# A priority for the split of the weights in a hybrid encoder step

## The chip, the cores and the metric

The kernel runs on one core of one Trainium2 chip. The metric is the device time of one execution in microseconds; a kernel's time is the median over several executions. The profile is one further execution, taken by the hardware profiler. The engines are called as the profile calls them: PE (TensorE) with its weight loads PEld, DVE (VectorE), ACT (ScalarE), POOL (GpSimd), SP (SyncE, which issues nearly all DMAs, all in one queue).

## The reference

One layer of a streaming encoder, for 2048 new frames with 16 learned meta tokens ahead of them and for 64 frames of a running stream:

```
h = RMSNorm(x); p = h @ W_in
o = concat[DiffAttn(p_A), RG-LRU(p_B), GLA(p_C)] @ W_out; x = x + o
h = RMSNorm(x)
x = x + (gelu(causal_dwconv3(h @ W_up)) * (h @ W_gate)) @ W_down
y = RMSNorm(x)
```

The model width is 1024, the width of the feed-forward part (FFN) 2816. Differential attention has 4 heads with two softmaxes each, under a mask that is causal by chunks of 64; RG-LRU and GLA are recurrences along the tokens. Everything is in float32.

## The kernel before

**Precision by splitting.** A float32 operand of a large product is split into two float32r parts, `hi` (the value rounded) and `lo` (the rest), and a product is three matmuls: hi·hi, lo·hi, hi·lo. So every weight tile of 128x1024 is split before it is used: it is loaded from HBM into `raw` (2 buffers), ACT rounds it into `whi` (line 154), and POOL (line 260, two of three) or DVE (line 160, one of three) subtracts to get `wlo`. `whi` and `wlo` have 3 buffers each.

**The list of weight pieces.** `parts` names the pieces in the order of their use: 86 for the projection W_in, then for each of three token groups the pieces of W_out, W_up, W_gate and W_down. The first two groups have 512 tokens each, the last 1104 in three blocks. In the first group a piece of W_out, W_up, W_gate or W_down is split as described, and its two halves are also stored to HBM (`WS`); in the second and third group they are loaded from `WS` and nothing is split. So there are 160 splits, 86 in the projection and 74 in the first group, and 148 pairs of loads from `WS`.

**When a piece is made ready.** `w_pump` is called between the products of the dense stream, `w_take` where a piece is used; both call `w_split`, which runs at most 3 pieces ahead of those used up (`NW`), so the buffer that a piece gets is that of the piece three places ahead of it in the list. `w_split` also calls `w_load`, the next load into `raw`.

**The order on the engines.** Three streams are written down interleaved, by estimated costs: the dense stream (projection, W_out, FFN), the attention and the recurrences. Each instruction has a priority number, the running `tc.cur_priority` at the place where it was written; a scheduler then orders each engine's instructions along a simulated time line, and of those that could start, the smallest number goes first. The streams get offsets by which they stand ahead: attention 30000, the recurrences 16000, the dense stream 0, the norms inside the dense stream 50000, the start of the program 100000 (`FIRST`). The last group runs alone, after the other streams. The streams end at:

```
    flow.run((dense(), 1875e3, 0), (attention(), 560e3, 30000),
             (recurrent(), 616e3, 16000))
```

**Names used below.** PE: `ps_w` the projection (lines 644, 646), `pd` W_out (line 1437) and W_down (line 1369), `pu` and `pg` W_up and W_gate (line 1302), `ps_sc` the attention scores (lines 1055, 1062), `ps_pt` transposes and `ps_o` the products with V (line 1169). The scores go through the minimum `NB` on DVE (line 1064) and the exponential `pc` on ACT (line 1065); `ph` is a transposed piece of the probabilities on ACT (line 154). `ck` and `ckr` are cached keys and their split, `e_gv` evictions of the projection, `Q`, `Kc`, `V` the loads of the attention.

Of the kernel before, what the change touches and what calls it, by code (L numbers as in the profile page):

```python
# [105 lines left out]
def f(ap):  # L106
    return ap.bitcast(F32)
# [31 lines left out]
def tile_hymba_step(ctx, tc, xT, xkT, cache_v, wi, wo, wu, wg, wd, par, sgla, c_msk, yT_p, yT_s, nkT_p, nv_p, lh_p, lc_p, gs_p, fc_p,  # L139
# [4 lines left out]
    def raw32(ap):  # L144
        return ap.bitcast(F32) if ap.dtype == F32R else ap

    def ld(out, in_):
        nc.sync.dma_start(out=raw32(out), in_=raw32(in_))

    def st(out, in_):  # L150
        nc.sync.dma_start(out=raw32(out), in_=raw32(in_))

    def rounded(out, in_, scale=1.0):
        nc.scalar.activation(out=out, in_=in_, func=AF.Copy, scale=scale)  # L154
# [4 lines left out]
    def minus(out, a, b):  # L159
        nc.vector.tensor_tensor(out, a, b, ALU.subtract)  # L160
# [75 lines left out]
    fresh = [i for i, x in enumerate(ids) if x is None or x not in ids[:i]]  # L236
    wq = {"load": 0, "split": 0, "used": 0, "raw": [], "ready": {}, "wait": 0, "n": 0}

    def w_load():
        if wq["load"] < len(fresh):  # L240
            _, src, n, _ = parts[fresh[wq["load"]]]
            t = wp.tile([P, D], F32, tag="raw", name="raw", bufs=NRAW)
            ld(out=t[:, :n], in_=src[:, :n])
            wq["raw"].append(t)
            wq["load"] += 1

    def w_split():
        i = wq["split"]
        key, _, n, w_ = parts[i]
        hi = wp.tile([P, D], F32R, tag="whi", name="whi", bufs=NW)  # L250
        lo = wp.tile([P, D], F32R, tag="wlo", name="wlo", bufs=NW)
        if i in fresh:
            if not wq["raw"]:
                w_load()
            t = wq["raw"].pop(0)
            rounded(hi[:, :n], t[:, :n])
            j = wq["n"]
            wq["n"] += 1
            if (j * 66) % 100 < 66 and j > 2 or j == 2:
                nc.gpsimd.tensor_tensor(out=lo[:, :n], in0=t[:, :n], in1=f(hi[:, :n]), op=ALU.subtract)  # L260
            else:
                minus(lo[:, :n], t[:, :n], f(hi[:, :n]))
            w_load()
            if w_ is not None and w_ in ids[i + 1:]:
                st(WS[w_][0, :, :n], hi[:, :n])
                st(WS[w_][1, :, :n], lo[:, :n])
        else:
            ld(out=hi[:, :n], in_=WS[w_][0, :, :n])
            ld(out=lo[:, :n], in_=WS[w_][1, :, :n])
        wq["ready"].setdefault(key, []).append((hi, lo))  # L270
        wq["split"] += 1

    def w_pump():
        wq["wait"] += 1
        if wq["wait"] % 2 == 0 and wq["split"] < min(len(parts), wq["used"] + NW):
            w_split()

    def w_take(key, n):
        while len(wq["ready"].get(key, ())) < n:
            w_split()  # L280
        return wq["ready"].pop(key)
# [7 lines left out]
    def setup():  # L289
        tc.cur_priority -= FIRST  # L290
        load_x(0, w_load)
        nc.scalar.dma_start(out=prm[:, :16], in_=par[:, :16])
        for _ in range(NRAW - 1):
            w_load()
        ld(out=prm[:, 16:], in_=par[:, 16:NPAR1])
        ld(out=prm2, in_=par[:, NPAR1:])
        make_identity(nc, ident)
        nc.gpsimd.memset(ones, 1.0)
        nc.gpsimd.memset(mhalf, -0.5)
        nc.scalar.activation(out=nlam, in_=mhalf[:, 0:1], func=AF.Square)  # L300
        tc.cur_priority += FIRST
# [1307 lines left out]
def build(inputs):  # L1609
    import concourse.bacc as bacc  # L1610

    nc = bacc.Bacc("TRN2", target_bir_lowering=False, num_devices=1)
    arrays, args = {}, []
    for name, a in _layout(inputs).items():
        arrays[f"in_{name}"] = a = np.ascontiguousarray(a)
        args.append(nc.dram_tensor(f"in_{name}", a.shape, mybir.dt.from_np(a.dtype), kind="ExternalInput").ap())
    for name, shape in _OUTS:
        args.append(nc.dram_tensor(f"out_{name}", shape, F32, kind="ExternalOutput").ap())
    with tile.TileContext(nc, schedule_with_timeline_sim=True) as tc:
        tile_hymba_step(tc, *args)  # L1620
    return nc, arrays
# [16 lines left out]
```

## Time and profile before

| | us |
|---|---|
| median of 3 runs | 2964.63 |
| lowest, highest | 2958.12, 2965.66 |
| the profiled execution | 2966.77 |
| its span, first to last instruction | 2965.0 |

| engine | busy, share of the span | instructions |
|---|---|---|
| PE | 2846.8 us, 96% | 16031 |
| PEld | 2508.9 us, 85% | 16031 |
| DVE | 1942.6 us, 66% | 3779 |
| ACT | 1140.1 us, 38% | 2589 |
| POOL | 864.2 us, 29% | 1212 |

The mean granted clock of PE is 0.979 of full speed. Busy time of PE is from a model of the ends of its matmuls, which overlap, so the start times of neighbouring matmuls tell the rate better than their durations. The stages, by the times at which their lines first and last run: the projection to about 800 us, the first token group from there to about 1490 us, the second to about 2035 us, the last to the end; the attention runs beside the first three, to about 1880 us; the last split starts at 1463.8 us.

### The profile page before, as it was taken

The page shows a single profiled execution, that of the slowest core. Times are in us where ns is not written, and L with a number is a line of the kernel's source. Part 1 is how long each engine was busy: PE and PEld are TensorE (multiplying, and loading weights), DVE is VectorE, ACT ScalarE, POOL GpSimd, SP SyncE. Part 2 cuts the span into 40 slices and gives each one's busy share as a digit, 9 for nine tenths or more (in the row PEclk, how much of TensorE's full clock was granted, in tenths as well). Part 3 has the DMA queues.
Part 4 walks back from the last instruction along what each step waited for, and adds up shares of the span by engine and source line. Part 5 has one row for each costly group of instructions (what it writes and reads, how often), then busy time and mean ns, then how long its engine had stood idle before and what let it go on. Part 6 is the DMA issues. An engine that isn't in the chain of part 4 may idle for free.

```text
span 2965.0 us, 44672 instructions
## 1 busy us (share of the span) xinstructions
PE 2846.8 (96%) x16031; PEld 2508.9 (85%) x16031; DVE 1942.6 (66%) x3779; ACT 1140.1 (38%) x2589; POOL 864.2 (29%) x1212
## 2 busy tenths in 40 slices
PE   7999999999899999999999999999999999999998
PEld 7988899989877787787787888888989998999997
DVE  7677685788879989979979766444454333333335
ACT  5454554555555455455444433111222121212122
POOL 4435534444435445444424221100110000000001
PEclk9999999999998999999998999999999999999998
DMA  7775574655796787787775565675222222222222
GB/s 233 208 210 148 175 225 139 196 181 188 237 336 216 250 261 246 230 261 266 262 265 171 188 204 193 243 287 197 73 86 86 86 86 86 86 86 86 86 86 105
DMA packets 277931, 537.44 MB, mean 181 GB/s; under 512 B 31014, under 2 KB 170030, under 8 KB 277710
## 3 DMA queue, kind: packets, MB, share of 16 engines
q1 hardware_dynamic: 277566, 534.58, 54.7%
q8 instruction: 127, 2.08, 0.3%
q14 instruction: 94, 0.77, 0.1%
q10 hardware_dynamic: 144, 0.01, 0.0%
HBM read 382.74 MB, written 151.76 MB: 180 GB/s over the span
## 4 chain that ended last, share of the span: by engine, by line
PE 72%; DVE 15%; DMA 5%; issue 3%; ACT 3%; POOL 2%; SPq 1%; POOLq 0%; ACTq 0%; DVEq 0%
PE pu L1302 15%; PE pd L1369 15%; PE pg L1302 14%; PE pd L1437 6%; PE ps_w L644 5%; PE ps_w L646 4%; PE ps_o L1169 3%; DVE pc L1103 3%; PE ps_sc L1062 2%; PE ps_sc L1055 2%; PE ps_pt L1154 2%; DVE NB L1064 1%; PE ps_r L894 1%; DMA raw<-in_wi 1%; DVE cc L1326 1%
## 5 line engine op out<-in xcount | busy, mean ns | idle before, releaser
L260 POOL TENSOR_TENSOR wlo<-raw,whi 128x1024 fp32r<-128x1024 f32 (+1 forms) x104 | 248.1, 2387 | 315.8 <-ACT whi L154 263.9
L1326 DVE SCALAR_TENSOR_TENSOR cc<-uh,prm,cc 128x512 f32<-128x512 f32 (+4 forms) x264 | 168.3, 645 | 256.4 <-ACT cc L1324 253.4
L1065 ACT ACTIVATE pc<-ps_sc,NB 128x512 f32<-128x512 f32 (+6 forms) x400 | 224.8, 563 | 285.7 <-DVE NB L1064 244.6
L1369 PE MATMUL pd<-gh,whi 128*128 128x512 f32 (+2 forms) x880 | 317.7, 363 | 12.3 <-DVE x L1375 10.6
L1375 DVE TENSOR_TENSOR x<-x,pd 128x512 f32<-128x512 f32 (+2 forms) x320 | 195.8, 617 | 200.3 <-PE pd L1369 199.0
L1302 PE MATMUL pu<-h2h,whi 128*128 128x512 f32 (+2 forms) x880 | 319.9, 364 | 7.1 <-ACT h2h L154 2.6
L1302 PE MATMUL pu<-h2l,whi 128*128 128x512 f32 (+2 forms) x880 | 318.0, 362 | 3.6 <-POOL h2l L443 2.7
L1302 PE MATMUL pu<-h2h,wlo 128*128 128x512 f32 (+2 forms) x880 | 317.4, 361 | 0.0
L1302 PE MATMUL pg<-h2h,whi 128*128 128x512 f32 (+2 forms) x880 | 315.4, 358 | 1.7 <-DMA whi<-WS 1.7
L1302 PE MATMUL pg<-h2h,wlo 128*128 128x512 f32 (+2 forms) x880 | 315.7, 359 | 0.0
L1302 PE MATMUL pg<-h2l,whi 128*128 128x512 f32 (+2 forms) x880 | 315.2, 358 | 0.0
L1369 PE MATMUL pd<-gl,whi 128*128 128x512 f32 (+2 forms) x880 | 314.0, 358 | 0.0
L1369 PE MATMUL pd<-gh,wlo 128*128 128x512 f32 (+2 forms) x880 | 313.9, 357 | 0.0
L1319 ACT ACTIVATE uh<-pu 128x336 f32<-128x336 f32 (+3 forms) x132 | 59.3, 465 | 556.9 <-PE pu L1302 556.3
L644 PE MATMUL ps_w<-hh,whi 128*128 128x384 f32 (+2 forms) x768 | 257.7, 338 | 16.1 <-ACT whi L154 10.9
L1064 DVE TENSOR_REDUCE NB<-ps_sc 128x1 f32<-128x512 f32 (+6 forms) x400 | 209.0, 529 | 79.8 <-PE ps_sc L1062 78.8
L644 PE MATMUL ps_w<-hl,whi 128*128 128x384 f32 (+2 forms) x768 | 258.2, 337 | 0.5 <-DVE hl L160 0.5
L644 PE MATMUL ps_w<-hh,wlo 128*128 128x384 f32 (+2 forms) x768 | 254.8, 334 | 0.3 <-DVE wlo L160 0.3
L157 POOL TENSOR_SCALAR gh<-cc 128x336 fp32r<-128x336 f32 (+3 forms) x132 | 68.4, 520 | 468.8 <-DVE cc L1339 376.2
L154 ACT ACTIVATE whi<-raw 128x1024 fp32r<-128x1024 f32 (+2 forms) x160 | 165.9, 1037 | 101.6 <-DMA raw<-in_wi 31.3
L1369 PEld LDWEIGHTS pd<-gh,whi 128*128 128x128 f32 x880 | 166.3, 189 | 36.9 <-DVE x L1375 13.1
L1302 PEld LDWEIGHTS pu<-h2h,whi 128*128 128x128 f32 x880 | 168.6, 192 | 30.0 <-issue 3.0
(330 smaller groups left out, 7126.4 us busy)
## 6 DMA issues: line engine op xcount, KB each, us to landing
wlo<-WS SPq DMA_DIRECT2D x148, 512.0 KB, 4.3
whi<-WS SPq DMA_DIRECT2D x148, 512.0 KB, 4.5
raw<-in_wi SPq DMA_DIRECT2D x74, 512.0 KB, 4.5
WS<-whi SPq DMA_DIRECT2D x74, 512.0 KB, 5.1
WS<-wlo SPq DMA_DIRECT2D x74, 512.0 KB, 6.3
Kc<-KHL SPq DMA_DIRECT2D x48, 512.0 KB, 5.3
V<-VHL SPq DMA_DIRECT2D x48, 512.0 KB, 5.2
Q<-QHL SPq DMA_DIRECT2D x64, 256.0 KB, 4.3
```

Source lines behind the costliest of these rows:

```text
L154: nc.scalar.activation(out=out, in_=in_, func=AF.Copy, scale=scale)
L260: nc.gpsimd.tensor_tensor(out=lo[:, :n], in0=t[:, :n], in1=f(hi[:, :n]), op=ALU.subtract)
L644: nc.tensor.matmul(ps[:, :n], lhsT=wx, rhs=hx, start=st_, stop=sp_)
L646: nc.tensor.matmul(ps[:n, :wd_], lhsT=hx, rhs=wx, start=st_, stop=sp_)
L1064: nc.vector.tensor_reduce(NB[:qw, ti, m, ci:ci + 1], ps[:qw, :kt_], AX.X, ALU.min)
L1065: nc.scalar.activation(out=pv_[m][:qw, :kt_], in_=ps[:qw, :kt_], func=AF.Exp, scale=-1.0, bias=NB[:qw, ti, m, ci:ci + 1], accum_out=SS[:qw ...
L1103: nc.vector.scalar_tensor_tensor(out=p0, in0=p0, scalar=u.R[:qw, ti, 0, ci:ci + 1], in1=p1, op0=ALU.mult, op1=ALU.add)
L1302: nc.tensor.matmul(ps[:, :n], lhsT=w_[wi_][:, k * P:(k + 1) * P], rhs=hx, start=(k == 0 and i3 == 0), stop=(k == KT - 1 and i3 == 2))
L1326: nc.vector.scalar_tensor_tensor(out=cc[:, :m], in0=uh[:, w:w + m], scalar=cw[w], in1=cc[:, :m], op0=ALU.mult, op1=ALU.add)
L1369: nc.tensor.matmul(ps[:, :n], lhsT=w_, rhs=g_[:, o:o + n], start=(j == 0 and i3 == 0), stop=(j == len(gts) - 1 and i3 == 2))
L1375: nc.vector.tensor_tensor(x2[b, ct], x2[b, ct], ps[:, :n], ALU.add)
L1437: nc.tensor.matmul(ps[:, :n], lhsT=w_, rhs=g_, start=(k == 0 and i3 == 0), stop=(k == KT - 1 and i3 == 2))
```

## The change

The priority number is lowered by 60000 while `w_split` runs, so all that it writes down (the rounding, the subtraction, the next load into `raw`, the stores to and the loads from `WS`) stands ahead of the attention, the recurrences and the norms, where before it stood at the dense stream's own place. What is computed, the buffers and the order in which the streams are written down stay the same.

```
+    AHEAD = 60000
...
     def w_split():
         i = wq["split"]
         key, _, n, w_ = parts[i]
+        tc.cur_priority -= AHEAD
         hi = wp.tile([P, D], F32R, tag="whi", name="whi", bufs=NW)
         lo = wp.tile([P, D], F32R, tag="wlo", name="wlo", bufs=NW)
         if i in fresh:
...
         else:
             ld(out=hi[:, :n], in_=WS[w_][0, :, :n])
             ld(out=lo[:, :n], in_=WS[w_][1, :, :n])
+        tc.cur_priority += AHEAD
         wq["ready"].setdefault(key, []).append((hi, lo))
         wq["split"] += 1
```

The scheduler makes a new order of this on all engines. Below, a row is a line of the program, the operation and its tiles; lines from 275 on are 5 higher in the changed program (1065 there is 1070).

Place 1: SP near the start of the program, about 45 us in. `XK<-ckr` stores split cached keys, `LGT<-e_lgt` stores results of the projection. Before:

```order
L148 DMA raw<-in_wi 128x816
L151 DMA XK<-ckr 64x2x512 x2
L148 DMA ck<-in_xkT 128x512
L148 DMA raw<-in_wi 128x544
L151 DMA LGT<-e_lgt 128x336
L148 DMA raw<-in_wi 128x1024
```

Now:

```order
L148 DMA raw<-in_wi 128x816
L151 DMA XK<-ckr 64x2x512
L148 DMA raw<-in_wi 128x544
L151 DMA XK<-ckr 64x2x512
L148 DMA ck<-in_xkT 128x512
L151 DMA LGT<-e_lgt 128x336
L148 DMA raw<-in_wi 128x1024
```

The weight load of 128x544 has gone ahead of one store and of the load of cached keys `ck`; the load of 128x1024 after it still follows the same store `LGT<-e_lgt`.

Place 2: ACT in the first token group, around the rounding of the piece of W_up for the eighth FFN tile (the second `whi<-raw` in each excerpt). `oS` and `osq` belong to GLA, `fr` and `oo` to the attention. Before:

```order
L154 ACTIVATE whi<-raw 128x1024
L1065 ACTIVATE pc,SS<-ps_sc,NB 128x512 x2
L154 ACTIVATE ph<-ps_pt 128x512
L1065 ACTIVATE pc,SS<-ps_sc,NB 128x512 x2
L917 ACTIVATE oS<-ps_r 128x256
L928 ACTIVATE osq<-oS 128x256
L154 ACTIVATE whi<-raw 128x1024
L154 ACTIVATE ph<-ps_pt 128x512
```

Now:

```order
L154 ACTIVATE whi<-raw 128x1024
L1070 ACTIVATE pc,SS<-ps_sc,NB 128x144 x2
L1085 ACTIVATE fr<-fr 128x4x4
L154 ACTIVATE oo<-oSs 128x256
L154 ACTIVATE ph<-ps_pt 128x512
L154 ACTIVATE whi<-raw 128x1024
L1070 ACTIVATE pc,SS<-ps_sc,NB 128x512 x2
L154 ACTIVATE ph<-ps_pt 128x512
L922 ACTIVATE oS<-ps_r 128x256
L933 ACTIVATE osq<-oS 128x256
L1070 ACTIVATE pc,SS<-ps_sc,NB 128x512 x2
```

The same rounding now has the four exponentials of 128x512 behind it that stood ahead of it.

Place 3: SP in the first token group, around two loads of weights. Before:

```order
L151 DMA WS_123<-wlo 128x1024
L148 DMA qk<-LGT 128x2x256
L148 DMA Kc<-KHL 128x2x144
L151 DMA OT<-lo 128x2x256
L151 DMA WS_124<-whi 128x1024
L148 DMA V<-VHL 128x4x256
L151 DMA OT<-lo 128x2x256
L148 DMA raw<-in_wg 128x1024
L151 DMA WS_124<-wlo 128x1024
L151 DMA WS_93<-whi 128x1024
L148 DMA raw<-in_wu 128x1024
```

Now:

```order
L151 DMA WS_123<-wlo 128x1024
L148 DMA V<-VHL 128x4x256
L151 DMA WS_124<-whi 128x1024
L148 DMA raw<-in_wg 128x1024
L151 DMA WS_124<-wlo 128x1024
L148 DMA qk<-LGT 128x2x256
L151 DMA OT<-lo 128x2x256 x2
L151 DMA WS_93<-whi 128x1024
L148 DMA Kc<-KHL 128x2x144
L148 DMA raw<-in_wu 128x1024
```

The loads `qk` and `Kc` have fallen behind three transfers of a split, `Kc` behind a fourth.

## Rows read from the trace of the kernel before

**Rows 1.** Stretches: length, busy (count) of PE, PEld, DVE, ACT, POOL; clock; DMA share; GB/s.

```profile
60.00:800.00 740.00, 700.41 (x4575) 661.35 (x4575) 557.18 (x1165) 376.87 (x945) 326.68 (x362) 0.98 0.62 187
800.00:1470.00 670.00, 631.75 (x3078) 513.82 (x3078) 594.74 (x1148) 349.39 (x812) 297.82 (x382) 0.96 0.79 262
1470.00:1900.00 430.00, 420.91 (x2107) 349.54 (x2106) 308.84 (x583) 166.65 (x384) 109.28 (x162) 0.98 0.59 199
```

**Rows 2.** Waits of PE, 60 to 800 us: us in total, times, longest.

```profile
PE ps_sc L1055 <- DMA Q<-QHL: 7.6, 4, 3.4
PE ps_sc L1055 <- ACT pc L1065: 6.8, 9, 1.4
PE ps_w L644 <- ACT whi L154: 4.1, 1, 4.1
```

**Rows 3.** Waits of PE, 800 to 1470 us, the four longest.

```profile
PE ps_sc L1055 <- ACT pc L1065: 11.8, 10, 4.1
PE pd L1369 <- DVE x L1375: 10.6, 6, 3.8
PE ps_o L1169 <- ACT ph L154: 2.7, 1, 2.7
PE pu L1302 <- DVE x L1375: 2.3, 1, 2.3
```

**Rows 4.** PE in time: start us, us, line, tiles [idle before <-what ended it].

```profile
1313.08 0.50 PE L1302 MATMUL pu<-h2h,whi 128*128 128x512 f32 x1 [2.26 <-DVE x L1375]
...
1314.55 0.63 PE L1302 MATMUL pu<-h2h,wlo 128*128 128x512 f32 x1
1314.97 0.63 PE L1302 MATMUL pu<-h2h,whi 128*128 128x512 f32 x1
...
1317.53 0.40 PE L1302 MATMUL pu<-h2h,whi 128*128 128x512 f32 x1
1317.77 0.39 PE L1302 MATMUL pu<-h2l,whi 128*128 128x512 f32 x1
```

**Rows 5.** PE, ACT, DVE in order of time: one split of the first token group.

```profile
1042.39 0.40 PE L1369 MATMUL pd<-gl,whi 128*128 128x512 f32 x1
...
1043.92 1.04 ACT L154 ACTIVATE whi<-raw 128x1024 fp32r<-128x1024 f32 x1
...
1045.00 1.23 DVE L160 TENSOR_TENSOR wlo<-raw,whi 128x1024 fp32r<-128x1024 f32 x1 [0.72 <-ACT whi L154]
...
1062.12 0.39 PE L1302 MATMUL pu<-h2h,whi 128*128 128x512 f32 x1
```

**Rows 6.** ACT groups, 800 to 1470 us: busy, mean ns; idle before and what ended it.

```profile
L1065 ACT ACTIVATE pc<-ps_sc,NB 128x512 f32<-128x512 f32 (+4 forms) x158 | 94.4, 598 | 109.9 <-DVE NB L1064 92.1 <-PE ps_pt L1154 16.7 <-DVE dg L861 0.4
L154 ACT ACTIVATE whi<-raw 128x1024 fp32r<-128x1024 f32 x72 | 76.0, 1055 | 32.1 <-PE pd L1369 15.8 <-PE pu L1302 12.0 <-PE pg L1302 1.6
```

**Rows 7.** SP, ACT and PE in order of time, 45 to 64 us.

```profile
45.91 0.54 SPq L148 DMA_DIRECT2D ck<-in_xkT  x1
46.56 0.84 SPq L148 DMA_DIRECT2D raw<-in_wi  x1
...
51.76 0.63 ACT L154 ACTIVATE ckr<-ck 128x512 fp32r<-128x512 f32 x1 [4.29 <-DMA ck<-in_xkT]
...
52.66 0.65 ACT L154 ACTIVATE whi<-raw 128x544 fp32r<-128x544 f32 x1
...
53.36 0.35 PE L646 MATMUL ps_w<-whi,hh 128*80 128x272 f32 x1 [1.12 <-ACT whi L154]
...
61.85 0.48 ACT L524 ACTIVATE e_gv<-ps_w,r 128x272 f32<-128x272 f32 x1
...
62.86 1.05 ACT L154 ACTIVATE whi<-raw 128x1024 fp32r<-128x1024 f32 x1
...
63.96 0.42 PE L644 MATMUL ps_w<-hh,whi 128*128 128x336 f32 x1 [4.10 <-ACT whi L154]
```

**Rows 8.** Waits of SP, 800 to 1470 us.

```profile
SPq L148 <- POOL wlo L260: 62.5, 26, 5.6
```

More of the change, by code (lines that the diff above doesn't have):

```diff
@@ L237, in tile_hymba_step @@
     wq = {"load": 0, "split": 0, "used": 0, "raw": [], "ready": {}, "wait": 0, "n": 0}
+    AHEAD = 60000
     def w_load():
@@ L249, in w_split @@
         key, _, n, w_ = parts[i]
+        tc.cur_priority -= AHEAD
         hi = wp.tile([P, D], F32R, tag="whi", name="whi", bufs=NW)
@@ L269, in w_split @@
             ld(out=lo[:, :n], in_=WS[w_][1, :, :n])
+        tc.cur_priority += AHEAD
         wq["ready"].setdefault(key, []).append((hi, lo))
```

## The prediction

> **What bounds the kernel.** I read the stretches first, then PE's waits by stretch, then the time line around single splits. PE is the bound. It is busy for 2846.8 of the 2965.0 us of the span, and in the three stretches that the attention shares with the dense stream it is busy for 700.41 of 740, 631.75 of 670 and 420.91 of 430 us [rows 1]: idle for 39.6, 38.3 and 9.1 us, 87.0 in all. DVE comes next, with 594.74 of 670 us in the first token group, while ACT has half of its time free and POOL more than half.
>
> An idle PE costs more than its idle time. After a wait of 2.26 us the starts of matmuls of 512 columns lie 0.42 us apart (1314.55 to 1314.97), and about 3 us later 0.24 us (1317.53 to 1317.77) [rows 4]: the clock stood at the lower of its two levels, 1.2 instead of 2.4 GHz. The mean clock of the three stretches, 0.98, 0.96 and 0.98 [rows 1], puts the loss at 0.02 x 740 + 0.04 x 670 + 0.02 x 430 = 50 us. So 87 + 50 = 137 us hang on waits in these stretches, and PE gets faster only if such a wait goes.
>
> **Is a split ever what PE waits for?** The change helps directly only there. From 60 to 800 us one wait for a rounded weight is left, 4.1 us long [rows 2]; the longer ones are for `Q` (7.6 us) and for the exponentials (6.8 us). From 800 to 1470 us, where 72 splits run, the large waits are for the exponentials (11.8 us in 10 waits), for DVE's addition into `x` (10.6 us) and for `ph` (2.7 us) [rows 3]. No weight is among them. One split shows why [rows 5]. Its buffer comes free with the matmul at 1042.39 us, ACT rounds it at 1043.92, DVE has `wlo` at 1045.00 + 1.23 = 1046.23, and PE first uses it at 1062.12: 15.9 us to spare. The rounding started 1.3 us after the start of the last reader of its buffer, so no priority can bring it forward by much more. What sets the time of a split is its three buffers, not its rank.
>
> **The change, part by part, against the profiled 2966.77 us.**
>
> *The start (place 1).* The load of 128x544 now goes ahead of `ck`. It was issued at 46.56 us, and its piece was rounded at 52.66, after `ckr`, which had waited for `ck` until 51.76 [rows 7]. ACT still has `ckr` ahead of that rounding, and `ck` is now issued after the load, whose own issue takes 0.84 us at most [rows 7]. So PE's wait of 1.12 us at 53.36 stays or grows by up to 0.84 us. The wait of 4.10 us at 63.96 is for the rounding at 62.86, which stands behind the eviction `e_gv` of 61.85; it still does, and its load still follows the same store. I take 0; the ends are -5.2 us (both waits go) and +0.8.
>
> *The splits on ACT, POOL and DVE (place 2).* No instruction is added. In the first token group one rounding (1055 ns each, 72 of them in the stretch [rows 6]) now stands ahead of four exponentials that stood ahead of it. As the split itself can't move by more than 1.3 us [rows 5], I read this the other way round: the attention slides back against the dense stream, by four exponentials of 598 ns [rows 6] or more. That costs nothing by itself, because the attention ends well before the kernel does: the last token group, 900 us long, runs alone. It costs or gains only where PE, whose instructions are in a fixed order too, finds an exponential later or earlier than it does now. The trace of before can't show that order's waits. I bound them by what PE waits for ACT in this stretch, 11.8 + 2.7 = 14.5 us [rows 3], which may all go or double; with the stretch's clock (26.8 us lost on 38.3 us idle, so 0.70 for each) that is 14.5 x 1.70 = 24.7 us either way. I take 0, since the nearest row, the spare 15.9 us of a split [rows 5], says that nothing here was late.
>
> *The queue of SP (place 3).* The next loads into `raw` and the stores to `WS` go ahead of loads of the attention. A load into `raw` waits for POOL to have read the buffer: 62.5 us in 26 waits in the stretch [rows 8], 2.4 us each, and `Kc` and `qk` now stand behind such a wait. `Kc` and `V` have two buffers each and no large wait of PE names them [rows 2, 3]; `Q` has one buffer and costs 7.6 us before 800 us [rows 2]. I take 0; the ends are 0 and +7.6 us, those waits doubled.
>
> *The second and third token group.* Nothing is split there; 148 pairs of loads move ahead in SP's queue. The last group has no attention to move past, so I take 0.
>
> The sum is 0: 2966.8 us for a profiled execution. The median of the runs lies 2.1 us below the profiled one, so I forecast **2964.6 us**. A measurement of this kernel can tell about 0.3% from no change, 8.9 us here.
>
> **The rivals.** *Faster.* PE runs out of dense work beside the attention because the scheduler, on its time line, had the splits ready late and put attention next; with the splits first, dense matmuls stand where PE now waits for exponentials. That takes out the 14.5 us on ACT and the clock's share: 2964.6 - 24.7 = **2940 us**. For it: the 11.8 us on the exponentials are PE's largest item in the stretch [rows 3]. Against it: a split has 15.9 us to spare [rows 5], so the dense work was there.
>
> *Slower.* ACT is blocked at the head of its queue. A rounding that comes before its buffer is free holds everything behind it, the exponentials above all. ACT sits idle for 32.1 us before these roundings even now, 15.8 and 12.0 us of it on PE's matmuls [rows 6]. If the four exponentials really wait behind the split, the waits of PE on ACT double: 2964.6 + 24.7 = **2989 us**. This decides once roundings reach the head of the queue more than the 1.3 us [rows 5] ahead of their release, and PE's next score matmul is due by then. For it: in place 2 four exponentials are passed, 2.4 us of ACT's work. Against it: the new order puts score matmuls later on PE as well. The Trainium skill ("PSUM — Partial Sum Buffer", Engine vs sequencer instructions) says that the queues of ScalarE, VectorE and GpSimdE are strict FIFO. By that rule every wait of a promoted rounding is passed on whole to what stands behind it; the trace agrees as far as the 32.1 us go, in which ACT had work queued behind the rounding [rows 6], and the rule would make this rival's 2989 us the forecast if the splits came early.
>
> *No effect at all*, the order staying as it is, is ruled out by the three places.
>
> **The chances.** No measurable change 0.41: no weight is late, and no operation is added. Faster by over 0.3% 0.32, slower by over 0.3% 0.27: the order of every engine changes in a part of the kernel with 137 us on waits, and a shift of a fifteenth of that is measurable. I put faster a little ahead, because early weights give the scheduler more to choose from. The range is that of the two rivals, **2940 to 2989 us**; more than that on either side I leave out with 2 in 10. The likeliest case by itself spans 2956 to 2973 us.
>
> **What would show it.** Right: no wait of PE on `whi` or `wlo` after 70 us; the rounding in the first token group still within about 2 us of the release of its buffer; 87 us of idle PE up to 1900 us within 10 us; the clock of the stretches as now. The faster rival would show the waits on `pc` from 800 to 1470 us well under 11.8 us and a clock above 0.96 there; the slower one, ACT's idle time before `whi` well over 32.1 us, the waits on `pc` over 20 us and a lower clock. Wrong altogether I would be if waits on DVE's additions into `x` (10.6 us now) change most, since the change moves one split in three on DVE, the engine with the least time free.

## The result, and the profile after

The changed kernel takes **2984.91 us** (median of 4 runs, 2981.07 to 2988.09), the kernel before 2965.14 us beside it: a ratio of 1.0064 on record, with a 95% interval from 1.0045 to 1.0083 (the quotient of the two medians by itself is 1.0067). It is slower by 0.64%. The forecast was no measurable change, and with it the likeliest case ended at 2973 us; the time lies inside the wide range, on the side to which I had given the smallest chance. Every line after 274 is 5 higher now.

The three stretches of [rows 1], and the stretch from 180 to 430 us that will matter, in the changed kernel (columns as there):

```profile
60.00:800.00 740.00, 697.50 (x4509) 657.45 (x4510) 551.09 (x1152) 369.02 (x928) 324.47 (x356) 0.97 0.62 185
800.00:1470.00 670.00, 631.80 (x3118) 515.97 (x3117) 588.48 (x1140) 349.24 (x809) 310.40 (x389) 0.97 0.78 260
1470.00:1900.00 430.00, 413.92 (x2067) 341.87 (x2066) 311.30 (x593) 170.44 (x396) 101.65 (x159) 0.96 0.59 200
180.00:430.00 250.00, 231.40 (x1437) 215.98 (x1436) 199.76 (x408) 127.51 (x337) 117.35 (x138) 0.96 0.61 179
```

The last of them in the kernel before:

```profile
180.00:430.00 250.00, 235.24 (x1520) 220.30 (x1518) 194.84 (x407) 131.20 (x345) 118.90 (x141) 0.99 0.64 191
```

PE is idle for 42.5, 38.2 and 16.1 us in the three stretches, 96.8 us in all where it was 87.0 before. The first token group, on which the prediction spent most of its words, is as it was: 631.80 us busy against 631.75, at a slightly higher clock. The loss lies ahead of it and behind it. From 180 to 430 us PE starts 1437 matmuls instead of 1520, with 3.8 us more of idle time and a clock of 0.96 instead of 0.99.

PE's waits of the changed kernel from 60 to 1900 us (us in total, times, longest):

```profile
PE ps_o L1174 <- DVE pl L160: 11.2, 8, 4.0
PE ps_sc L1060 <- DMA Q<-QHL: 11.0, 6, 3.3
PE ps_sc L1060 <- ACT pc L1070: 10.1, 15, 2.0
PE ps_on L1198 <- POOL dgt L157: 8.0, 3, 4.3
PE pd L1374 <- DVE x L1380: 7.0, 6, 2.5
PE ps_r L813 <- ACT tt L731: 6.4, 4, 2.2
PE ps_o L1174 <- DVE oSs L1200: 5.7, 2, 4.2
```

and of the kernel before in the same stretch:

```profile
PE ps_sc L1055 <- ACT pc L1065: 18.7, 20, 4.1
PE pd L1369 <- DVE x L1375: 10.6, 6, 3.8
PE ps_sc L1055 <- DMA Q<-QHL: 10.4, 5, 3.4
PE ps_w L644 <- ACT whi L154: 4.1, 1, 4.1
```

The exponentials `pc`, by which both rivals were to be told, gave back 8.6 us. The waits on `pl`, `dgt`, `oSs` (attention) and `tt` (RG-LRU), small or absent among the waits before, took that and more. No single wait explains the change.

**A measure of what PE loses.** The order of PE's instructions is another one, so equal times and equal counts can't be compared directly. I therefore gave every kind of matmul (output, shape, type) a price: the 30th percentile of the time from one start to the next, over the traces of all kernels here. The whole program comes to the same sum by these prices in every trace, to 1 us. What PE has lost at a moment is that moment less the prices of all that it has started. It is an estimate: with the matmuls put into kinds in another way, single entries below move by up to 2 us. The changed kernel loses, beside the kernel before, -2.8 us up to 180 us, **+10.2 us from 180 to 430 us**, and +7.9 us from there to the end: 15.3 us, beside the 14.1 us by which the profiled spans differ. (The medians differ by 19.8 us. The profiled execution of the changed kernel, 2981.07 us, is the lowest of its four, so some 5 us stand in no trace.) The start is the small gain that the prediction allowed for: the waits of 1.12 and 4.10 us of [rows 7] are 1.69 and 2.52 now.

### The profile page after: what moved, and what is told of

It is laid out like the page before. It is cut to its first block, busy times and chain, and to the rows that moved or that the text cites. A ratio compares the mean times of both kernels' runs of the same rounds, so it can differ in the third digit from the quotient of the medians.

```text
span 2979.1 us, 44679 instructions
## 1 busy us (share of the span) xinstructions
PE 2848.9 (96%) x16031; PEld 2508.7 (84%) x16031; DVE 1938.3 (65%) x3779; ACT 1139.3 (38%) x2589; POOL 867.5 (29%) x1212
## 4 chain that ended last, share of the span: by engine, by line
PE 69%; DVE 18%; DMA 7%; issue 3%; ACT 3%; POOL 1%; SPq 1%; POOLq 0%; ACTq 0%; DVEq 0%
PE pd L1374 15%; PE pu L1307 15%; PE pg L1307 13%; PE ps_w L649 6%; PE pd L1442 6%; PE ps_o L1174 3%; PE ps_w L651 3%; DVE pc L1108 3%; PE ps_sc L1067 2%; PE ps_pt L1159 2%; DVE BD L894 2%; PE ps_sc L1060 2%; DVE NB L1069 1%; PE ps_r L899 1%; DVE y L443 1%
## 5 line engine op out<-in xcount | busy, mean ns | idle before, releaser
L1331 DVE SCALAR_TENSOR_TENSOR cc<-uh,prm,cc 128x512 f32<-128x512 f32 (+4 forms) x264 | 162.2, 622 | 258.0 <-ACT cc L1329 254.7
L1307 PEld LDWEIGHTS pu<-h2h,whi 128*128 128x128 f32 x880 | 167.6, 191 | 25.2 <-ACT h2h L154 3.8
```

What stands on the lines that cost most here:

```text
L1307: nc.tensor.matmul(ps[:, :n], lhsT=w_[wi_][:, k * P:(k + 1) * P], rhs=hx, start=(k == 0 and i3 == 0), stop=(k == KT - 1 and i3 == 2))
L1331: nc.vector.scalar_tensor_tensor(out=cc[:, :m], in0=uh[:, w:w + m], scalar=cw[w], in1=cc[:, :m], op0=ALU.mult, op1=ALU.add)
```

## Experiments

### Which part of the priority

e1 gives the priority to the splits alone, e2 to the loads from `WS` alone, e3 to the projection's pieces alone, e4 to those of the first token group alone.

```
 e1  ahead = AHEAD if i in fresh else 0
 e2  ahead = AHEAD if i not in fresh else 0
 e3  ahead = AHEAD if key[0] == "in" else 0
 e4  ahead = AHEAD if key[0] != "in" and key[1] == 0 else 0
+        tc.cur_priority -= ahead
...
+        tc.cur_priority += ahead
```

> The priority is kept for the pieces that are split (the projection and the first token group), and taken back for the loads from WS (second and third group). Theory 1, the loads from WS that moved ahead in SP's queue hold up loads of the attention at the start of the second group, where the changed kernel lost 11 us between 1541 and 1604 us: 11 us or more come back, about 2972 us or less. Theory 2, the splits of the first two stages push the attention back and the loss comes from there: no change against the changed kernel, 2981 to 2988 us. Theory 3, any new order of this size shifts the sum of PE's waits by some 10 to 20 us in either direction and this one happened to be a slow one: the order on PE is nearly that of the changed kernel, so 2975 to 2990 us as well.

Measured: 2987.28 us, 1.0058 (1.0041 to 1.0075). From 180 to 430 us it loses 9.9 us, afterwards 13.7.

> The priority for the loads from WS alone; the splits stand where they stood before. Theory 1 (loads from WS): about 2976 us or more. Theories 2 and 3: the order on PE is nearly that of the kernel before, so 2960 to 2970 us.

Measured: 2969.81 us, 1.0011 (0.9995 to 1.0027); 0.2 us and -6.3 us.

> The priority for the 86 pieces of the projection alone. Theory 2: a part of the loss only, that of the projection, where the changed kernel was 8 us behind at the end of the stage but 2 us when the first group began: 2965 to 2975 us. Theory 3: another new order of all that follows, so anything from 2950 to 2990 us, and the places of the loss are others than in the changed kernel. Theory 1: 2965 us.

Measured: 2981.74 us, 1.0039 (1.0025 to 1.0052); 10.0 us and 7.4 us.

> The priority for the 74 pieces that are split in the first token group alone. Theory 2: the rest of the loss, 2970 to 2980 us, with ACT idle longer before its roundings (40 us in the changed kernel against 32 before). Theory 3: anything from 2950 to 2990 us, with the first 800 us as in the kernel before. Theory 1: 2965 us.

Measured: 2975.99 us, 1.0025 (1.0015 to 1.0036); -0.5 us and 9.7 us.

My first theory came from the one long wait that is new in the second group. There the pair of loads from `WS` stands ahead of the load of `qk` in SP's queue, and DVE waits for that load. SP, DVE, POOL and PE of the changed kernel, in order of time:

```profile
1574.40 0.32 SPq L148 DMA_DIRECT2D wlo<-WS  x1
1575.15 0.32 SPq L148 DMA_DIRECT2D whi<-WS  x1
1575.57 0.37 SPq L148 DMA_DIRECT2D qk<-LGT  x1
...
1581.97 0.29 DVE L814 TENSOR_SCALAR qk<-qk 128x256 f32<-128x256 f32 x1 [2.27 <-DMA qk<-LGT]
...
1582.55 0.15 DVE L1191 COPY r<-ps_on 128x2 f32<-128x2 f32 x1
...
1583.86 0.72 POOL L157 TENSOR_SCALAR dgt<-ident,r 128x128 f32<-128x128 f32 x2
...
1584.63 1.22 PE L1198 MATMUL ps_on<-dgt,ones 128*128 128x256 f32 x2 [4.28 <-POOL dgt L157]
```

The copy of `r`, which needs nothing of `qk`, stands behind it on DVE, POOL makes `dgt` from `r`, and PE idles for 4.28 us. The chain is real, but it isn't what the change costs: e1, without any priority for the loads from `WS`, is as slow as the changed kernel, and e2, with that alone, shows no loss. What e1 and e3 share with the changed kernel is the projection. It is not the whole of it: e4, which leaves the projection alone, is slower by 0.25% through what comes after 430 us.

### The same change in other orders

The total of the attention in the table of streams (560e3) sets how densely it is written between the pieces of the dense stream. Four other totals, without the priority (c1, c3, c5, c7) and with it (c2, c4, c6, c8), give four more pairs; nothing of what is computed changes.

```
-    flow.run((dense(), 1875e3, 0), (attention(), 560e3, 30000),
+    flow.run((dense(), 1875e3, 0), (attention(), 555e3, 30000),
```

(c1 and c2; 565e3 in c3 and c4, 550e3 in c5 and c6, 570e3 in c7 and c8.)

> The kernel before, with the attention's total in the interleaving of the streams at 555e3 for 560e3: no priority changes, but some 4,200 rows of PE's order differ from before, about as many as under the change (4,900). Theory 3 (any new order shifts the time): anything from 2950 to 2990 us. Theory 2 (the splits ahead of the attention are what costs): 2960 to 2970 us.

Measured: 2967.94 us, 1.0004 (0.9987 to 1.0020).

> The changed kernel with the same pace, 555e3. Theory 2: slower than the kernel before at the same pace by 12 to 25 us. Theory 3: the difference to it has either sign.

Measured: 2964.90 us, 0.9993 (0.9980 to 1.0007).

> The kernel before with 565e3 for 560e3, a second order of equal meaning. Theory 3: anything from 2950 to 2990 us. Theory 2: 2960 to 2970 us.

Measured: 2951.44 us, 0.9951 (0.9936 to 0.9966): faster than both kernels.

> The changed kernel with 565e3. Theory 2: slower than the kernel before at the same pace by 12 to 25 us. Theory 3: the difference to it has either sign.

Measured: 2976.12 us, 1.0029 (1.0016 to 1.0042).

> The kernel before with 550e3 for 560e3. Theory 3 alone (any new order shifts the time): 2950 to 2990 us, as likely above as below the kernel with the priority at this pace. Theory 2 on top of it: below that kernel by 5 to 20 us.

Measured: 2968.54 us, 1.0006 (0.9993 to 1.0019).

> The changed kernel with 550e3. Theory 3 alone: either side of the kernel before at this pace. Theory 2 on top of it: above it by 5 to 20 us.

Measured: 2966.35 us, 1.0000 (0.9987 to 1.0013).

> The kernel before with 570e3 for 560e3. Theory 3 alone: 2950 to 2990 us. Theory 2 on top of it: below the kernel with the priority at this pace by 5 to 20 us.

Measured: 2966.33 us, 0.9995 (0.9983 to 1.0007).

> The changed kernel with 570e3. Theory 3 alone: either side of the kernel before at this pace. Theory 2 on top of it: above it by 5 to 20 us.

Measured: 2971.86 us, 1.0015 (0.9998 to 1.0032).

With the priority less without it, the ratios of the five pairs differ by -0.0006 (550), -0.0011 (555), +0.0064 (560, the case itself), +0.0078 (565) and +0.0020 (570): 0.0029 on average with a standard error of 0.0018. By the whole time alone, the loss could be the luck of one order. The measure of PE's losses says more. From 180 to 430 us the four kernels with the priority lose 12.5, 10.2, 8.6 and 9.8 us, like the changed kernel, e1 and e3; the four without it -1.4, -0.1, 4.9 and -2.8 us. What comes after 430 us has no such pattern.

These are not five independent tests of the stretch, though. The other totals deal another order to PE only later. Row by row in the traces, PE's order in e1, e3, c2 and c4 is that of the changed kernel up to 430 us, in c8 up to 428 us. In e2, e4, c1 and c3 it is that of the kernel before up to 430 us, in c7 up to 419 us. The middle stretch of these kernels compares two orders, run again and again. Only the total 550e3 deals a new order inside it, from 281 us on. There the kernel without the priority (c5, first row) and the one with it (c6) come out alike, in the same stretch in which the kernel before (third row) and the changed kernel (fourth) differ:

```profile
281.00:430.00 149.00, 141.64 (x906) 134.12 (x905) 107.73 (x227) 76.22 (x184) 68.71 (x80) 0.98 0.60 183
281.00:430.00 149.00, 141.38 (x905) 133.63 (x904) 111.68 (x233) 75.90 (x186) 68.20 (x81) 0.99 0.61 185
281.00:430.00 149.00, 143.87 (x942) 135.01 (x940) 112.16 (x231) 77.91 (x193) 70.10 (x78) 1.00 0.64 196
281.00:430.00 149.00, 141.01 (x888) 131.81 (x887) 117.41 (x231) 75.50 (x186) 69.85 (x81) 0.98 0.61 181
```

From 281 to 430 us c5 loses about 4.8 us and c6 about 3.9 beside the kernel before, the changed kernel and the others with its order 6.0 to 7.9. So the loss repeats from run to run for the order that this change makes; that the priority would cost as much in another order is not shown.

### Which instruction of the split

At first I looked for the cause where SP's queue and PE meet in this stretch. In the changed kernel a weight load is issued right ahead of the two loads of `Q`, and PE waits for them (SP, then PE):

```profile
396.57 0.42 SPq L148 DMA_DIRECT2D raw<-in_wi  x1
397.08 1.28 SPq L148 DMA_DIRECT2D Q<-QHL  x2
...
404.16 0.47 PE L1060 MATMUL ps_sc<-Kc,Q 128*128 128x512 f32 x1 [1.98 <-DMA Q<-QHL]
```

`Q` takes 6.3 us to land there by the view of DMA issues, behind 512 KB of weights. (That is no long time for it: the median of such loads up to 440 us is 6.8 us in the kernel before and 6.2 in the changed one.) So the next four runs took the instructions of the split apart. f1 leaves the load into `raw` at the dense stream's own rank, f2 promotes that load alone, f3 is the changed kernel with the same 60000 for the two loads of `Q`, f4 the kernel before with that alone.

```
 f1          minus(lo[:, :n], t[:, :n], f(hi[:, :n]))
+        tc.cur_priority += AHEAD
         w_load()
+        tc.cur_priority -= AHEAD
 f2 the reverse: the two new lines with the signs changed, and none around the rest
 f3, f4
+    tc.cur_priority -= 60000
     for half in range(2):
         ld(out=Q[64 * half:64 * half + 64, :, :, :nq],
...
+    tc.cur_priority += 60000
```

> As the changed kernel, but the next load into raw stands at the dense stream's own rank again; rounding, subtraction and the transfers of WS keep the priority. Measured against the work that PE has done, the seven kernels with the priority in the projection lost between 180 and 430 us 8.6 to 12.5 us more than the kernel before, the controls without it -2.8 to +4.9. Theory 4 (the stretch loses by the load of 512 KB that goes directly ahead of Q's loads at 397 us, and by a wlo that DVE has ahead of pl at 258 us): PE's wait of 2.0 us on Q near 404 us is gone, and the stretch loses about 3 us less, +5 to +8. Theory 3 (any new order shifts the waits): the loss of the stretch is anywhere between -3 and +5, like the controls'. Whole time 2960 to 2985 by either.

Measured: 2982.27 us, 1.0061 (1.0040 to 1.0083); 1.0 us lost from 180 to 430 us, 20.1 us afterwards.

> Only the next load into raw has the priority. Theory 4: the wait on Q near 404 us stays (2 us, with a lower clock behind it, 3 us in all), and the one on pl near 261 us goes back to 0.9 us or less, so that the stretch from 180 to 430 us loses +2 to +5 us. Theory 3: the loss of the stretch is between -3 and +5 us with other waits than these two. Whole time 2955 to 2980.

Measured: 2978.90 us, 1.0044 (1.0029 to 1.0059); 13.5 us and 12.4 us.

> As the changed kernel, but the two loads of Q get the same 60000, so that no weight load goes ahead of them in SP's queue. Theory 4: Q's loads land in under 6 us near 400 us, PE's wait on Q there falls from 2.0 to below 0.7 us, the stretch from 180 to 430 us loses 5 to 8 us instead of 10, and PE's waits on Q in the whole run fall from 11.0 to below 8 us. Theory 3: the whole order moves again, and the stretch and the whole time (2960 to 2985) can come out either way.

Measured: 2969.59 us, 1.0005 (0.9993 to 1.0017); -0.9 us and 8.2 us. PE's waits on `Q` from 60 to 1900 us come to 7.1 us.

> The kernel before with the 60000 for the two loads of Q alone; 12 rows of SP's order differ and none on PE, DVE or ACT. It prices SP's order by itself: PE's waits on Q (10.4 us in the kernel before) fall by 0 to 4 us where a transfer stood ahead of Q, and the time is 2958 to 2966. Where Q's loads wait for the last reader of their only buffer, nothing changes: within 0.2% of before.

Measured: 2967.85 us, 1.0002 (0.9992 to 1.0012); -1.3 us and 1.1 us. PE's waits on `Q`: 9.1 us.

The row from 180 to 430 us of f1, of f2 and of f3:

```profile
180.00:430.00 250.00, 233.77 (x1509) 218.14 (x1508) 196.20 (x408) 129.62 (x342) 117.48 (x140) 0.99 0.64 189
```

```profile
180.00:430.00 250.00, 228.73 (x1409) 213.25 (x1408) 194.82 (x397) 127.41 (x337) 115.19 (x138) 0.95 0.61 178
```

```profile
180.00:430.00 250.00, 236.22 (x1537) 221.01 (x1535) 194.07 (x411) 130.05 (x344) 119.72 (x140) 0.99 0.64 191
```

f1 and f3 have their clock back at 0.99 and, within 17, the count of the kernel before (1520); f2 has a lower clock than the changed kernel and fewer matmuls still. The promoted load alone makes the loss of this stretch, and it is gone when the load is not promoted (f1) or when `Q` is promoted with it (f3). It does not make the loss of the whole time alone: f1 loses next to nothing here (1.0 us) and is as slow as the changed kernel at the end.

The programs say how far the load's rank reaches. Up to about 680 us (some 4,000 matmuls) f2 has the changed kernel's order on PE word for word and f1 that of the kernel before; f3 differs from the kernel before in some tens of rows there, from 375 us on, the changed kernel in over a thousand. With the subtraction at its old rank the changed program is the same on every engine, so that part of the priority does nothing. The first difference between f3 and the changed kernel, on any engine, is one weight load at 149 us. SP in the kernel before:

```profile
150.03 1.24 SPq L148 DMA_DIRECT2D Q<-QHL  x2
151.32 0.60 SPq L148 DMA_DIRECT2D Kc<-XK  x1
...
152.75 0.45 SPq L148 DMA_DIRECT2D raw<-in_wi  x1
```

in the changed kernel:

```profile
148.44 0.58 SPq L148 DMA_DIRECT2D Q<-QHL  x1
149.07 0.59 SPq L148 DMA_DIRECT2D raw<-in_wi  x1
149.71 0.58 SPq L148 DMA_DIRECT2D Q<-QHL  x1
150.34 0.60 SPq L148 DMA_DIRECT2D Kc<-XK  x1
```

and in f3:

```profile
148.22 1.24 SPq L148 DMA_DIRECT2D Q<-QHL  x2
149.57 0.54 SPq L148 DMA_DIRECT2D raw<-in_wi  x1
150.15 0.44 SPq L148 DMA_DIRECT2D Kc<-XK  x1
```

With the load between the two halves of `Q`, the scheduler puts the scores of that `Q` ten rows further back on PE, behind matmuls of the projection, and everything behind them falls in another way. In time the load itself holds the second half up by 0.6 us. What costs 10 us is the order that follows: f3 sends the same load almost as early (149.57 us) and loses nothing.

So theory 4 held in that the load's place beside `Q` is the switch, and fell in its road. Theory 3 is not ruled out: the switch gives one other order, and that this order is a slower one may be chance. I had the wait at 404 us down as the main cost, and the wait on `pl` near 261 us as the work of a promoted `wlo`; f1 was to keep 5 to 8 us and f2 to lose 2 to 5. They measured 1.0 and 13.5: the wait on `pl` belongs to the order as well, and f2 loses more than any other with only 1.5 us of waits on `Q`. PE's waits from 180 to 430 us, on average over the kernels that lose there (8) and those that don't (12, the kernel before among them):

| PE waits for | 8 that lose, us | 12 that don't, us |
|---|---|---|
| ACT `tt` (RG-LRU) | 4.5 | 0.5 |
| DVE `pl` at `ps_pt` | 4.5 | 2.2 |
| DMA `Vx` | 1.8 | 0.0 |
| DMA `Q` | 3.6 | 3.9 |
| ACT `e_lgt` at `ps_w` | 1.6 | 2.6 |
| all | 20.9 | 13.2 |

Each group is for the most part one order of PE. On average the waits on `Q` are the same (in the changed kernel itself they are 6.2 us, in the kernel before 3.4); RG-LRU's are not. One of them in the changed kernel (ACT, then PE):

```profile
361.46 1.28 ACT L731 ACT_TABLE_LOAD   x1
362.76 0.47 ACT L731 ACTIVATE tt<-ps_r,hb 128x256 f32<-128x256 f32 x1
...
363.29 0.39 PE L813 MATMUL ps_r<-ident,gvr 128*16 128x128 f32 x2 [2.19 <-ACT tt L731]
```

and the same matmul in the kernel before:

```profile
375.92 0.47 ACT L726 ACTIVATE tt<-ps_r,hb 128x256 f32<-128x256 f32 x1
...
376.45 0.39 PE L808 MATMUL ps_r<-ident,gvr 128*16 128x128 f32 x2 [0.39 <-ACT tt L726]
```

Both have four table loads of 1283 ns on ACT in the stretch, and one right ahead of this `tt`; in the changed kernel PE's next transpose comes sooner than ACT is done.

### Another total for the attention

g1 is c4 with `Q` promoted, as f3 was the changed kernel with it; g2 is c3 with it, as f4 was the kernel before (edit as in f3).

> The changed kernel with the attention's total 565e3 in the table of streams (c4: 1.0029, and 10.2 us lost between 180 and 430 us), with the 60000 for the two loads of Q as in f3. Theory 4 (the loads into raw that pass Q's loads in SP's queue cost about 10 us there): the stretch loses -3 to +2 us beside the kernel before, as its sister without the priority does (c3: -0.1), and the first 3000 rows of PE's order are c3's but for 78. Theory 3: the stretch keeps a loss like that of c4, or takes another of 5 us or more. For the rest of the run both allow 10 us either way: 2945 to 2980.

Measured: 2966.15 us, 0.9996 (0.9981 to 1.0012); -0.2 us from 180 to 430 us, 4.3 us afterwards.

> The fastest kernel so far (c3, 2951.44, without the priority) with the 60000 for Q's two loads: the same order on PE in the first 3000 rows. Both theories: no loss between 180 and 430 us. If c3's gain is the chance of one order, this one, whose later rows differ in 2705 places, lies back at 2955 to 2972; if Q's place is worth something by itself, below 2951.

Measured: 2985.63 us, 1.0059 (1.0041 to 1.0077); -0.7 us and 25.2 us.

g1 repeats f3: c4's 10.2 us in the stretch are gone, and so is its loss in the whole time. On PE g1 has f3's order up to 482 us, so for the stretch this is f3 once more. g2 shows what c3's 2951.44 us were: with PE's order the same in the first 3000 rows, but another one later, the gain of 0.5% became a loss of 0.6%.

All kernels by PE's losses beside the kernel before, in us:

| | up to 180 us | 180 to 430 us | after 430 us |
|---|---|---|---|
| load into `raw` ahead, `Q` not: changed, e1, e3 | -2.8, -1.9, -0.9 | 10.2, 9.9, 10.0 | 7.9, 13.7, 7.4 |
| the same in other orders: c2, c4, c6, c8 | -1.1, -1.7, -0.9, -3.9 | 12.5, 10.2, 8.6, 9.8 | -10.4, -1.8, -9.6, -4.2 |
| that load alone: f2 | 0.6 | 13.5 | 12.4 |
| no priority there: e2, e4 | -0.8, 1.9 | 0.2, -0.5 | -6.3, 9.7 |
| none at all, other orders: c1, c3, c5, c7 | -1.2, -1.8, 0.5, -1.0 | -1.4, -0.1, 4.9, -2.8 | 9.6, -12.3, 1.6, 1.3 |
| load at its old rank: f1 | -2.3 | 1.0 | 20.1 |
| `Q` ahead as well: f3, g1 | -1.6, -0.1 | -0.9, -0.2 | 8.2, 4.3 |
| `Q` ahead alone: f4, g2 | 0.8, 0.8 | -1.3, -0.7 | 1.1, 25.2 |

The middle column has two groups, 8.6 to 13.5 us (8 kernels, mean 10.6) and -2.8 to 4.9 us (11 kernels, mean -0.2), told apart by whether the load into `raw` has the higher rank and `Q` has not. How well one order repeats can be read there too: the kernels that have the order of the kernel before up to 430 us lie between -1.4 and 1.0 us, those with the changed kernel's between 9.9 and 13.5. The last column has no groups: 1.9 us on average in the first and 5.7 in the second, with a standard deviation of about 10 us in each. Each entry is from one execution; those of f2 and g2 are the slowest of their kernels (2990.89 and 2990.19 us, with medians of 2978.90 and 2985.63), so this column holds the spread of executions as well as that of orders.

## Why the prediction was wrong

**The step that failed is place 3, the queue of SP.** It priced the loads into `raw` that go ahead of loads of the attention at 0, on the ground that `Kc` and `V` have two buffers, and kept the doubled waits on the single-buffered `Q`, +7.6 us, as an end. The load's rank against `Q` decides which order PE gets from 154 us on (f1, f2, f3, g1), and with the one that the change makes PE loses 10.6 us from 180 to 430 us. That is a little above the step's end, though not by the waits on `Q`, which on average over those kernels are no longer than in the others (3.6 and 3.9 us). Two things were missing. The step asked only who would wait for the transfer, when here the load's place moved the order that the scheduler builds on it; and it looked only at the first token group, where 26 waits of SP on POOL had caught the eye [rows 8]. But 86 of the 160 splits are the projection's, and all of that stage was costed by its first 64 us.

In the changed kernel the 10 us come out of the rows like this: from 180 to 430 us PE's idle time goes from 14.8 to 18.6 us and the clock from 0.99 to 0.96, worth 0.03 x 250 = 7.5 us; idle time and clock make 11.3 us, beside the 10.2 measured. Why this order meets more waits of the recurrences is not taken further here, and whether a load between `Q`'s halves would cost as much in another order stays open (c5 and c6). f4 shows that moving `Q` alone on SP, without the load, is worth no more than 1.3 us there.

**The remainder** of the case, 7.9 us after 430 us, is not shown to come from the change. Kernels with the load ahead spread from -10.4 to 13.7 us there, those without it from -12.3 to 25.2. The prediction gave a new order a cost of 0 with a likeliest case of 2956 to 2973 us; the spread after 430 us alone, about 10 us either way, is wider than that, and it too was missing. The load's place makes about 0.35% (10.6 of 2965 us) of the 0.64% that the case shows. What makes the rest is open: f1, without the load's rank, is as slow (1.0061) by what it loses after 430 us.

**Point by point.**

*No weight is late*: right but for little. PE's waits on `whi` and `wlo` from 70 to 1900 us are one of 0.40 us, at a score, and one of 1.74 us, where the kernel before has none; the splits gained nothing, since they had next to nothing to gain. One reading in the working is off: the rounding of [rows 5] starts 1.5 us after the start of its buffer's last reader (1043.92 - 1042.39), not 1.3, which changes nothing that hangs on it. Nor does that split stand for all: over the 74 of the first group, with each last reader taken from the program, the lag is 1.0 us in the median and up to 10.4 us in the kernel before, 0.6 and up to 12.2 us in the changed one.

*The start*, 0 with ends of -5.2 and +0.8: -2.8 us up to 180 us, of which 1.0 us lies in the two waits of [rows 7].

*The exponentials*, 14.5 us either way: PE's waits on `pc` from 800 to 1470 us fell from 11.8 to 5.3 us. The faster rival's sign came, and no gain with it, since the waits on other results of the attention and the recurrences rose by as much.

*The slower rival*: ACT's idle time before the roundings rose as it said, from 32.1 to 40.2 us; the rows of ACT from 800 to 1470 us now:

```profile
L1070 ACT ACTIVATE pc<-ps_sc,NB 128x512 f32<-128x512 f32 (+4 forms) x156 | 92.2, 591 | 124.9 <-DVE NB L1069 104.4 <-PE ps_pt L1159 11.8 <-DVE pc L1108 6.5
L154 ACT ACTIVATE whi<-raw 128x1024 fp32r<-128x1024 f32 x73 | 76.9, 1054 | 40.2 <-PE pd L1374 14.9 <-PE pd L1442 12.6 <-issue 6.9
```

but the waits on `pc` did not double, they halved. The time came out near its 2989 us by another road, so that this nearness is luck. The Trainium skill ("PSUM — Partial Sum Buffer", Engine vs sequencer instructions) has the queues of ScalarE, VectorE and GpSimdE strictly first in, first out; the chain from `qk` to `dgt` on DVE agrees with it, 2.27 us of waiting in front and 4.28 us of idle PE behind. It tells that a wait is handed on, and not whether PE then has other work.

*The signs*: 87 us of idle PE within 10 us held (96.8), and still the time left the band of 0.3%. With the clock's share of 0.7 us for each idle one, which the prediction itself had worked out, 10 us of idle time are 17 us: the sign was wider than the claim. The clocks were to stay as they were; they are 0.97, 0.97 and 0.96 where they were 0.98, 0.96 and 0.98.

*Additions into `x`*: 7.0 us now, and not what changed most.

## What to carry to other kernels

A higher rank for a producer moves everything that it issues, and the transfers may matter where the arithmetic does not: compare the order of every queue in every stage in which the step runs. Here it was a load put between two others that one consumer needs. Where PE is 96% busy and a scheduler writes the order, price a new order by a spread and not by 0; a few kernels that compute the same in another order give that spread, and a comparison of one pair can't tell a loss of 0.3% from luck. Compare progress by the work done, stretch by stretch: that showed 10 us in 250 where the whole times of five pairs showed nothing sure. And before such kernels are counted as separate tests, see whether their orders differ in the stretch that is compared: here eight kernels without a difference are one order, measured eight times. Among the versions run, c3 beat both kernels (2951.44 us), but as the luck of one order.

## What the hardware showed unasked

How much one short wait costs is not told by its length. PE of the changed kernel, in order of time:

```profile
256.79 0.70 PE L899 MATMUL ps_r<-BD,EK 128*128 128x256 f32 x2 [1.32 <-DVE att L903]
...
261.04 0.39 PE L1159 MATMUL ps_pt<-ident,pc 128*16 128x128 f32 x2 [1.80 <-DVE pl L160]
...
261.45 0.52 PE L649 MATMUL ps_w<-hh,whi 128*128 128x384 f32 x1
261.77 0.52 PE L649 MATMUL ps_w<-hl,whi 128*128 128x384 f32 x1
...
265.69 0.34 PE L649 MATMUL ps_w<-hh,whi 128*128 128x384 f32 x1
265.87 0.34 PE L649 MATMUL ps_w<-hl,whi 128*128 128x384 f32 x1
```

and the same wait in the kernel before:

```profile
264.33 0.38 PE L1154 MATMUL ps_pt<-ident,pc 128*16 128x128 f32 x2 [0.91 <-DVE pl L160]
...
266.54 0.34 PE L644 MATMUL ps_w<-hh,wlo 128*128 128x384 f32 x1
266.71 0.33 PE L644 MATMUL ps_w<-hh,whi 128*128 128x384 f32 x1
```

After a wait of 1.80 us, 4 us behind another of 1.32, matmuls of 384 columns start 0.32 us apart, and 0.18 us apart again by 265.69: the granted clock was half of full speed, 1.2 GHz, from 261.4 to 264.8 us. After the wait of 0.91 us they stay at 0.17 us, and the granted clock is 1.00 from 263 to 270 us. Twice the wait cost more than twice the time: 1.80 us of waiting and about 1.7 us by the clock, against 0.91.
